# A chunked recurrence in four strands, with its group norm done chunk by chunk

## The chip, the cores and the metric

The kernel runs on one core of a Trainium2 chip. The metric is the device time of one execution in microseconds (us). Of the core's engines, PE (TensorE) multiplies matrices, DVE (VectorE) and ACT (ScalarE) do the elementwise work, POOL (GpSimd) does a few small powers, and SP issues the DMAs. Each engine takes its instructions strictly in the order in which the compiled program lists them for it.

## The reference

A decoder trunk of two layers over 1024 tokens of width 1024, in float32. The first layer mixes time with a linear recurrence (RWKV-7), the second with differential attention; each is followed by a gated feed-forward layer with a short convolution. What the change touches is the recurrence of the first layer and the group norm on its output:

```
def step(state, inp):
    rt, wt, kt, vt, at, bt = inp
    sa = jnp.einsum('bhvk,bhk->bhv', state, at)
    state = state * wt[:, :, None, :] + sa[..., None] * bt[:, :, None, :] + vt[..., None] * kt[:, :, None, :]
    y = jnp.einsum('bhvk,bhk->bhv', state, rt)
    return state, y
...
mean = jnp.mean(o, axis=-1, keepdims=True)
var = jnp.mean(jnp.square(o - mean), axis=-1, keepdims=True)
o = ((o - mean) * lax.rsqrt(var + GN_EPS)).reshape(bsz, s, d) * ln_w + ln_b
bonus = jnp.sum(rh * kh * r_k.astype(jnp.float32), axis=-1, keepdims=True) * vh
o = o + bonus.reshape(bsz, s, d)
return (o * g).astype(h.dtype) @ w_o, v_first
```

There are 16 heads of 64. The state of a head is 64 x 64.

## The kernel before

The 1024 tokens of the recurrence are cut into 8 tiles of 128, and a tile into 4 chunks of 32. Within a chunk the recurrence is solved in matrix form, so only the state goes from chunk to chunk. A tile has six parts, each a generator that yields between its steps:

- `wkv_e` (10 steps): loads, decays, keys. It writes the buffers `AS` (two) and `KB` (one).
- `wkv_a` (7 steps): first four steps, one for each chunk, that form the products `KB` x `AS` on PE (L625) and mask them on DVE (L631, L636); then the inverse of a 32 x 32 triangle for each head and chunk: a run of 28 small DVE instructions (L653, L655), transposes that give `TT` (L662), and two products on PE (L671, L677) with an ACT copy between them. It is called "the solve" here.
- `wkv_x`, "the turn" (4 steps): DVE scales `KD` by the decay (L688), PE multiplies it by `KB` (L696), ACT copies the result into `KD` (one buffer, which the chain reads).
- `wkv_c`, "the chain" (4 chunks x 3 steps): the products with the state, L723, L732, L745 and L753, with an ACT copy behind each. L753 gives the output, which goes to `YT`.
- `wkv_p` (4 steps): group norm of the whole tile (square on ACT L768, sum on DVE L770, power on POOL L307, scaling on DVE L773), transposes on PE (L778), bias and gate (L782 to L793), store.

`wkv` sets their order: `wkv_e` and `wkv_a` of the next tile (front, 17 steps) are woven one step for one with `wkv_c` and `wkv_p` of the present one (back, 16 steps), and when both are done the turn of the next tile follows alone. All products of e, a, x and p go through three PSUM banks (tag `w`), those of the chain through two others.

Beside all this runs a filler, the generator `beside`: the second half of the projections (matmuls `ps<-xh`), then the output projection of finished tiles (`ps<-oh`), then `ffn_pre`, the up-projection of the feed-forward layer for the first half (`u<-h`). The driver in `trunk` gives it 0.4 of a step for each step of the recurrence while the projections last and until tile 4 is done, then 0.75 of a step. What is left is drained after the recurrence, together with the output projection of the second half.

A scheduler then fixes the order on each engine: mostly program order, with instructions of neighbouring steps moved past each other.

Of the kernel before, what the change touches and what calls it, by code (L numbers as in the profile page):

```python
# [9 lines left out]
F32 = mybir.dt.float32  # L10
F32R = mybir.dt.float32r
BF16 = mybir.dt.bfloat16
AF = mybir.ActivationFunctionType
ALU = mybir.AluOpType
AX = mybir.AxisListType
PSUM = bass.MemoryType.PSUM

P = 128
S = 1024
D = 1024  # L20
NK = 8
# [6 lines left out]
GN_EPS = 64e-5  # L28
# [45 lines left out]
def EG(nc, i):  # L74
    return nc.gpsimd if i in EP else nc.vector
# [10 lines left out]
class Trunk:  # L86
# [421 lines left out]
    def wkv_e(self, T):  # L508

        nc = self.nc  # L510
# [4 lines left out]
        wk, we = self.wk, self.we  # L515
        cst = self.wcst
# [7 lines left out]
        bv = T.bv = wk.tile([P, NK, P], F32, tag="bv", name="bv", bufs=2)  # L524
        nc.sync.dma_start(bv, self.rkv_d[2, half, :, :, qs].rearrange("j p t -> p j t"))
        AS = T.AS = wk.tile([P, 2, NK, 4, 64], F32, tag="AS", name="AS", bufs=2)
        KB = T.KB = wk.tile([P, NK, 4, 64], F32, tag="KB", name="KB")
        PC = T.PC = wk.tile([P, 2, NK], F32, tag="PC", name="PC", bufs=2)
        inv = wk.tile([P, 16], F32, tag="inv", name="inv")

# [5 lines left out]
        for jh in range(2):  # L536
# [29 lines left out]
            sq = et("tz")  # L566
# [20 lines left out]
                nc.tensor.matmul(bo[:, jj * P:(jj + 1) * P], self.bork[:, 4 * jh + jj, :], rk[:, jj, :], start=True, stop=True)  # L587
            for b in range(2):
                nc.vector.tensor_copy(PC[:, b, js], E1[:, b::2, 64])
            kbd = KB[:, js, :, :].rearrange("p j c t -> p (j c) t")  # L590
            EG(nc, 2).tensor_tensor(out=kbd[:, :, 0:32], in0=c4(kp), in1=c4(E3), op=ALU.mult)
            for hh in range(2):
# [22 lines left out]
    def wkv_a(self, T):  # L615

        nc, wk, cst = self.nc, self.wk, self.wcst
        AS, KB, NA = T.AS, T.KB, self.NA
        for c in range(4):
            Ap = self.wtile_ps()  # L620
            for j in range(NK):
                for hh in range(2):
                    r = slice(64 * hh, 64 * hh + 64)
                    o = slice(64 - 64 * hh, 128 - 64 * hh)
                    nc.tensor.matmul(Ap[o, j * 64:(j + 1) * 64], KB[r, j, c, :], AS[r, hh, j, c, :], start=True, stop=True)  # L625
            Av = Ap.rearrange("p (j t) -> p j t", j=NK)
            for hh in range(2):
                u0 = 96 - 64 * hh
                for jp in range(2):
                    g = 3 - 2 * hh - jp  # L630
                    nc.vector.tensor_tensor(  # L631
                        out=NA[32 * g:32 * g + 32, 4 * c:4 * c + 4, :], in0=Av[u0:u0 + 32, jp::2, 0:32],
                        in1=cst[u0:u0 + 32, W_NM:W_NM + 32].unsqueeze(1).to_broadcast([32, 4, 32]), op=ALU.mult)
            for hh in range(2):
                o = slice(64 - 64 * hh, 128 - 64 * hh)
                nc.vector.tensor_tensor(out=AS[o, hh, :, c, :], in0=Av[o], in1=cst[o, W_AM:W_AM + 64].unsqueeze(1).to_broadcast([64, NK, 64]), op=ALU.mult)  # L636
            yield

        even, first = cst[:, W_M0:W_M0 + 1], cst[:, W_M0 + 1:W_M0 + 2]
        tr = lambda t: t.rearrange("p s (b t) -> p t (s b)", t=16)  # L640
        n2 = lambda: wk.tile([P, 16, CH], F32, tag="NT", name="NT", bufs=2)
        Nn = wk.tile([P, 16, CH], F32, tag="Nn", name="Nn")
        NT = n2()
        nc.vector.transpose(NT, tr(NA))
        M = wk.tile([P, 16, 16], F32, tag="M", name="M")
        nc.vector.scalar_tensor_tensor(out=M, in0=NT[:, :, 0:16], scalar=even, in1=NT[:, :, 16:32], op0=ALU.mult, op1=ALU.add)
        nc.vector.transpose(Nn, NA)
        tmp = wk.tile([P, 64], F32, tag="tmp", name="tmp")

        for j in range(1, 15):  # L650
            a = 15 - j
            tv = tmp[:, :a * j].rearrange("p (x y) -> p x y", x=a)
            nc.vector.tensor_tensor(out=tv, in0=M[:, j + 1:, j:j + 1].to_broadcast([P, a, j]),  # L653
                                    in1=M[:, j:j + 1, :j].to_broadcast([P, a, j]), op=ALU.mult)
            nc.vector.tensor_tensor(out=M[:, j + 1:, :j], in0=M[:, j + 1:, :j], in1=tv, op=ALU.add)  # L655
        nc.vector.memset(M.rearrange("p a b -> p (a b)")[:, ::17], 1.0)

        DX = n2()
        nc.vector.tensor_scalar(out=DX[:, :, 0:16], in0=M, scalar1=even, scalar2=None, op0=ALU.mult)
        nc.vector.tensor_tensor(out=DX[:, :, 16:32], in0=M, in1=DX[:, :, 0:16], op=ALU.subtract)  # L660
        TT = T.TT = wk.tile([P, 16, CH], F32, tag="TT", name="TT", bufs=2)
        nc.vector.transpose(tr(TT), DX)  # L662
        DN = n2()
        nc.vector.transpose(DN, TT)
        yield
        ps = [self.wtile_ps(), self.wtile_ps()]
        Rs = wk.tile([P, 256], F32, tag="Rs", name="Rs")
        for i in range(16):
            for g in range(4):
                r = slice(32 * g, 32 * g + 32)  # L670
                nc.tensor.matmul(ps[0][r, 16 * i:16 * i + 16], Nn[r, i, :], TT[r, i, 16:32], start=True, stop=True)  # L671
        nc.scalar.copy(Rs, ps[0][:, 0:256])
        yield
        for i in range(16):
            for g in range(4):
                r = slice(32 * g, 32 * g + 32)
                nc.tensor.matmul(ps[1][r, 16 * i:16 * i + 16], DN[r, i, :], Rs[r, 16 * i:16 * i + 16], start=True, stop=True)  # L677
        nc.vector.scalar_tensor_tensor(out=TT[:, :, 16:32], in0=ps[1][:, 0:256].rearrange("p (s t) -> p s t", t=16), scalar=first,
                                       in1=TT[:, :, 16:32], op0=ALU.mult, op1=ALU.add)
        yield  # L680

    def wkv_x(self, T):
# [7 lines left out]
        for c in (0, 2, 1, 3):  # L690
            Kp = self.wtile_ps()
            for j in range(NK):
                for hh in range(2):
                    r = slice(64 * hh, 64 * hh + 64)
                    o = slice(64 - 64 * hh, 128 - 64 * hh)
                    nc.tensor.matmul(Kp[o, j * 64:(j + 1) * 64], T.KB[r, j, c, :], KD[r, hh, c, j, :], start=True, stop=True)  # L696
            for hh in range(2):
# [12 lines left out]
    def wkv_c(self, T):  # L710

        nc, wk = self.nc, self.wk
        AS, TT, KD = T.AS, T.TT, self.KD
        fl = lambda t: t.rearrange("p a b -> p (a b)")
        YT = T.YT = wk.tile([P, 4, 256], F32, tag="YT", name="YT")
        self.wkv_v(T.ti, 0)
        for c in range(4):
            s0, s1 = self.svu[c % 2], self.svu[1 - c % 2]
# [31 lines left out]
            for jj in range(2):  # L750
                for hh in range(2):
                    for j4 in range(4):
                        nc.tensor.matmul(Yp[32 * j4:32 * j4 + 32, (jj * 2 + hh) * 64:(jj * 2 + hh) * 64 + 64],  # L753
                                         AS[:, hh, jj * 4 + j4, c, 32:64], s0[:, hh, jj * 4 + j4, :], start=True, stop=True)
            nc.scalar.copy(YT[:, c, :], Yp[:, 0:256])
            yield

    def wkv_p(self, T):

        nc, wk, we = self.nc, self.wk, self.we  # L760
        YT, bv = T.YT, T.bv
        gl0, gl1 = T.lot[2], T.lot[3]
        ptile = self.wtile_ps
        y3 = YT.rearrange("p c (h v) -> p (c h) v", v=64)
        var = wk.tile([P, 16], F32, tag="st", name="st")
        bcs = lambda a: a.unsqueeze(2).to_broadcast([P, 16, 64])
        sq = we.tile([P, 16, 64], F32, tag="gq", name="gsq")
        nc.scalar.activation(sq, y3, AF.Square)  # L768
        yield
        nc.vector.tensor_reduce(out=var, in_=sq, axis=AX.X, op=ALU.add)  # L770
        self.rstd_cols(var, var, 64, GN_EPS)
        yield
        nc.vector.tensor_tensor(out=y3, in0=y3, in1=bcs(var), op=ALU.mult)  # L773
        on = we.tile([P, NK, P], F32, tag="gq", name="on")
        for jj in range(2):
            tp = ptile()
            for c in range(4):
# [18 lines left out]

    def wkv(self):

        class Tile:
            pass  # L800
        ts = []
        for i in range(8):
            t = Tile()
            t.ti = i
            ts.append(t)
        self.tiles_done = 0

        def front(t):
            yield t.ti // 4 + 1
            for g in (self.wkv_e(t), self.wkv_a(t)):  # L810
                for _ in g:
                    yield 0

        def back(t):
            for g in (self.wkv_c(t), self.wkv_p(t)):
                for _ in g:
                    yield 0
            self.tiles_done += 1

        def turn(t):  # L820
            for _ in self.wkv_x(t):
                yield 0
        yield from front(ts[0])
        yield from turn(ts[0])
        for i, t in enumerate(ts):
            yield from weave(back(t), front(ts[i + 1]) if i < 7 else iter(()), 16, WF)
            if i < 7:
                yield from turn(ts[i + 1])


    def x_open(self, half, right=False):
# [741 lines left out]
END = object()  # L1573
# [7 lines left out]
def weave(a, b, na, nb):  # L1581

    da = db = 0
    la = lb = True
    while la or lb:
        if la and (not lb or da * nb <= db * na):
            v = next(a, END)
            la = v is not END
            da += 1
        else:  # L1590
            v = next(b, END)
            lb = v is not END
            db += 1
        yield 0 if v is END else v
# [79 lines left out]
WF = 17  # L1674
# [186 lines left out]
```

## Time and profile before

| | |
|---|---|
| median of 3 runs | 3306.48 us (3298.51 to 3312.58) |
| the profiled execution | 3304.96 us, its span 3303.2 us |
| the recurrence | from about 320 to 1240 us of the span |
| PE, DVE, ACT busy over the span | 91%, 65%, 37% |
| mean granted clock of PE | 0.943 of 2.4 GHz |

The span is the time from the first instruction to the last. A wait is idle time of an engine, put down to the instruction that ended it. The granted clock has two levels, 1.2 and 2.4 GHz; a mean of 0.89 says that 22% of a stretch ran at the lower one.

### The profile page before, as it was taken

To read this page: it belongs to the slowest core of one execution; us is meant where nothing else is said; L and a number is where in the kernel's file an instruction comes from. 1 tells how busy PE (TensorE), PEld (TensorE's weight loads), DVE (VectorE), ACT (ScalarE), POOL (GpSimd) and SP (SyncE) were. 2 spreads that over 40 slices of the span, in tenths; PEclk is the share of its full clock that TensorE was granted. 3 is DMA by queue.
4 is the path that set the end of the run, shared out by engine and by line. 5 is a ranking of instruction groups with operands and counts; after the bars stand their busy time and mean duration, and the time that the engine had idled before them with its cause. 6 is when DMAs were issued, how large, how long until landed. Compare 5 with 4: busy or idle time off the path is not lost.

```text
span 3303.2 us, 53483 instructions
## 1 busy us (share of the span) xinstructions
PE 3004.2 (91%) x21607; PEld 2419.4 (73%) x21607; DVE 2152.5 (65%) x3752; ACT 1228.2 (37%) x2165; POOL 84.1 (3%) x50
## 2 busy tenths in 40 slices
PE   5988888987899997899999889898889999999997
PEld 2574667776677775788888678787678888888885
DVE  2656778566777855687777676777656655555555
ACT  3634455554454543322223333444333221222123
POOL 0000000000000000000000000000000000000000
PEclk7999899988899998999999899899899999999998
DMA  7363344343433337454443445445552111111111
GB/s 244 113 201 111 98 125 122 115 116 109 117 116 106 100 105 241 153 159 138 141 153 121 149 134 141 136 124 153 151 177 97 52 51 39 58 45 51 39 45 51
DMA packets 441402, 387.85 MB, mean 117 GB/s; under 512 B 42832, under 2 KB 369856, under 8 KB 440130
## 3 DMA queue, kind: packets, MB, share of 16 engines
q1 hardware_dynamic: 438850, 380.23, 38.3%
q8 instruction: 170, 2.79, 0.4%
q10 hardware_dynamic: 2304, 4.20, 0.3%
q14 instruction: 78, 0.64, 0.1%
HBM read 298.74 MB, written 83.49 MB: 116 GB/s over the span
## 4 chain that ended last, share of the span: by engine, by line
PE 68%; DVE 14%; DMA 6%; issue 6%; ACT 4%; POOL 1%; SPq 0%; DVEq 0%; POOLq 0%; ACTq 0%
PE u L109 9%; PE u L110 8%; PE u L111 8%; PE d L109 5%; PE d L111 5%; PE d L110 5%; PE ps L109 5%; PE ps L110 4%; PE ps L111 4%; DMA agw<-in_ada_w_dram 2%; PE wp L696 1%; PE sc L1539 1%; PE cp L745 1%; DVE AS L636 1%; PE tp L1466 1%
## 5 line engine op out<-in xcount | busy, mean ns | idle before, releaser
L109 PE MATMUL u<-h,whl 128*128 128x512 f32 x1408 | 561.8, 399 | 12.7 <-DVE mu L1089 10.0
L110 PE MATMUL u<-h,whl 128*128 128x512 f32 x1408 | 554.3, 394 | 6.2 <-DVE whl L164 6.2
L111 PE MATMUL u<-h,whl 128*128 128x512 f32 x1408 | 552.7, 393 | 0.0
L1134 DVE SCALAR_TENSOR_TENSOR x<-d,mod,x 128x512 f32<-128x512 f32 x352 | 261.8, 749 | 180.7 <-PE d L111 180.6
L109 PEld LDWEIGHTS u<-h,whl 128*128 128x128 f32 x1408 | 265.7, 189 | 73.5 <-ACT h L1090 10.2
L110 PEld LDWEIGHTS u<-h,whl 128*128 128x128 f32 x1408 | 265.8, 189 | 63.3 <-DVE whl L164 8.7
L111 PEld LDWEIGHTS u<-h,whl 128*128 128x128 f32 x1408 | 265.6, 189 | 59.6
L100 ACT CAST whl<-raw 128x1024 fp32r<-128x1024 f32 x140 | 143.9, 1042 | 433.6 <-PE d L111 421.5
L1046 DVE SCALAR_TENSOR_TENSOR a<-u,cwc,a 128x511 f32<-128x511 f32 (+1 forms) x132 | 122.0, 924 | 258.7 <-ACT a L1045 258.6
L109 PE MATMUL d<-hid,whl 128*128 128x512 f32 x704 | 280.1, 398 | 8.3 <-ACT hid L100 6.0
L110 PE MATMUL d<-hid,whl 128*128 128x512 f32 x704 | 277.3, 394 | 0.0
L111 PE MATMUL d<-hid,whl 128*128 128x512 f32 x704 | 275.4, 394 | 0.0
L1045 ACT ACTIVATE a<-u,cwc 128x512 f32<-128x512 f32 (+1 forms) x132 | 121.5, 921 | 390.9 <-PE u L111 390.5
L164 DVE TENSOR_TENSOR whl<-wraw,whl 128x512 fp32r<-128x512 f32 x232 | 158.0, 685 | 123.5 <-ACT whl L163 121.1
L163 ACT CAST whl<-wraw 128x512 fp32r<-128x512 f32 x232 | 142.7, 618 | 248.5 <-PE ps L111 102.9
L109 PE MATMUL ps<-xh,whl 128*128 128x512 f32 x384 | 162.7, 424 | 9.8 <-ACT xh L100 8.2
L101 DVE TENSOR_TENSOR whl<-raw,whl 128x1024 fp32r<-128x1024 f32 x140 | 168.9, 1217 | 4.0 <-ACT whl L100 3.8
L109 PEld LDWEIGHTS d<-hid,whl 128*128 128x128 f32 x704 | 133.2, 189 | 44.4 <-ACT hid L100 9.3
L111 PE MATMUL ps<-xl,whl 128*128 128x512 f32 x384 | 156.7, 409 | 4.6 <-DVE xl L101 4.3
L110 PE MATMUL ps<-xh,whl 128*128 128x512 f32 x384 | 156.4, 408 | 4.4 <-DVE whl L164 4.4
L111 PEld LDWEIGHTS d<-hid,whl 128*128 128x128 f32 x704 | 133.2, 189 | 30.3 <-DVE hid L101 1.6
L110 PEld LDWEIGHTS d<-hid,whl 128*128 128x128 f32 x704 | 133.3, 189 | 26.8
(279 smaller groups left out, 5863.9 us busy)
## 6 DMA issues: line engine op xcount, KB each, us to landing
raw<-in_ffn_w_up_dram SPq DMA_DIRECT2D x88, 512.0 KB
wraw<-in_a_w_rkv_dram SPq DMA_DIRECT2D x96, 256.0 KB
agw<-in_ada_w_dram SPq DMA_DIRECT2D x96, 256.0 KB
wraw<-in_ffn_w_up_dram SPq DMA_DIRECT2D x88, 256.0 KB
raw<-in_ffn_w_down_dram SPq DMA_DIRECT2D x44, 512.0 KB
agw<-in_ada_w_dram SPq DMA_DIRECT2D x128, 128.0 KB
rkv_d<-st SPq DMA_DIRECT2D x48, 256.0 KB
wraw<-in_a_w_o_dram SPq DMA_DIRECT2D x48, 256.0 KB
```

The costliest lines, as they stand in the source:

```text
L100: nc.scalar.copy(h, src)
L101: nc.vector.tensor_tensor(out=l, in0=src, in1=h.bitcast(F32), op=ALU.subtract)
L109: nc.tensor.matmul(ps, wh, xh, start=first, stop=False)
L110: nc.tensor.matmul(ps, wl, xh, start=False, stop=False)
L111: nc.tensor.matmul(ps, wh, xl, start=False, stop=last)
L163: nc.scalar.copy(wt[:, 0], raw)
L164: self.low().tensor_tensor(out=wt[:, 1], in0=raw, in1=wt[:, 0].bitcast(F32), op=ALU.subtract)
L636: nc.vector.tensor_tensor(out=AS[o, hh, :, c, :], in0=Av[o], in1=cst[o, W_AM:W_AM + 64].unsqueeze(1).to_broadcast([64, NK, 64]), op=ALU.mult)
L696: nc.tensor.matmul(Kp[o, j * 64:(j + 1) * 64], T.KB[r, j, c, :], KD[r, hh, c, j, :], start=True, stop=True)
L1045: nc.scalar.activation(a, u, AF.Identity, bias=c[3], scale=c[2])
L1046: nc.vector.scalar_tensor_tensor(out=a[:, 1:], in0=u[:, :n - 1], scalar=c[1], in1=a[:, 1:], op0=ALU.mult, op1=ALU.add)
L1134: nc.vector.scalar_tensor_tensor(out=xs, in0=ps, scalar=gate[:, j:j + 1], in1=xs, op0=ALU.mult, op1=ALU.add)
```

## The change

The inverse becomes a generator of its own, `wkv_s` (3 steps), and `wkv` runs four strands in turn, a step of each that can go: back (chain, then `wkv_p`), solve, turn and front (`wkv_e`, then the four steps of `wkv_a`). A strand goes on as soon as what it needs is done or its buffer is free; the front of a tile may start two steps before the turn of the tile ahead of it has released `KB`. The norm moves into the chain: after each chunk its 128 x 256 outputs are squared, summed, raised to -1/2 and scaled. The steps of a tile fall from 38 to 35, and with them the filler's share.

```diff
@@ wkv_e
-        KB = T.KB = wk.tile([P, NK, 4, 64], F32, tag="KB", name="KB")
...
+            if jh == 0:
+                KB = T.KB = wk.tile([P, NK, 4, 64], F32, tag="KB", name="KB")
@@ wkv_a
             yield
+
+    def wkv_s(self, T):
+
+        nc, wk, cst, NA = self.nc, self.wk, self.wcst, self.NA
@@ wkv_c
+        var = wk.tile([P, 4, 4], F32, tag="st", name="st")
+        on = T.on = self.we.tile([P, NK, P], F32, tag="gq", name="on")
+        bv4 = lambda t: t.rearrange("p (h v) -> p h v", v=64)
...
             nc.scalar.copy(YT[:, c, :], Yp[:, 0:256])
+
+            sq = bv4(on[:, 2 * c:2 * c + 2, :].rearrange("p a b -> p (a b)"))
+            nc.scalar.activation(sq, bv4(YT[:, c, :]), AF.Square)
+            nc.vector.tensor_reduce(out=var[:, c], in_=sq, axis=AX.X, op=ALU.add)
+            self.rstd_cols(var[:, c], var[:, c], 64, GN_EPS)
+            nc.vector.tensor_tensor(out=bv4(YT[:, c, :]), in0=bv4(YT[:, c, :]), in1=var[:, c].unsqueeze(2).to_broadcast([P, 4, 64]),
+                                    op=ALU.mult)
             yield
@@ wkv_p
-        sq = we.tile([P, 16, 64], F32, tag="gq", name="gsq")
-        nc.scalar.activation(sq, y3, AF.Square)
-        yield
-        nc.vector.tensor_reduce(out=var, in_=sq, axis=AX.X, op=ALU.add)
-        self.rstd_cols(var, var, 64, GN_EPS)
-        yield
-        nc.vector.tensor_tensor(out=y3, in0=y3, in1=bcs(var), op=ALU.mult)
@@ wkv
-        yield from front(ts[0])
-        yield from turn(ts[0])
-        for i, t in enumerate(ts):
-            yield from weave(back(t), front(ts[i + 1]) if i < 7 else iter(()), 16, WF)
-            if i < 7:
-                yield from turn(ts[i + 1])
+        def front():
+            for i, t in enumerate(ts):
+                while done["p"] < i - 1 or self.halves < i // 4 + 1:
+                    yield False
+                for n, _ in enumerate(self.wkv_e(t)):
+                    yield True
+
+                    while n == 1 and done["x"] < i:
+                        yield False
+                done["e"] += 1
...
+        def turn():
+            for i, t in enumerate(ts):
+                while done["e"] <= i or done["c"] < i:
+                    yield False
+                for _ in self.wkv_x(t):
+                    yield True
+                done["x"] += 1
+
+        def solve():
+            for i, t in enumerate(ts):
+                while done["a"] <= i:
+                    yield False
...
+        def back():
+            for i, t in enumerate(ts):
+                while done["s"] <= i or done["x"] <= i:
+                    yield False
...
+        live = [back(), solve(), turn(), front()]
```

The first place at which the orders are compared is PE's queue at the end of tile 3 (`AS,KB` are the products of `wkv_a` for tile 4, `YT` the transposes of `wkv_p`, `TT,Nn` and `Rs,NT` the solve, `KD,KB` the turn, `lot` with `w2x` or `a2a` the first products of the next front, `ps<-oh` the filler). Before:

```order
L625 MATMUL wp<-AS,KB 64x64 x32
L723 MATMUL cp<-svu_1980,AS 32x64 x16
L778 MATMUL wp<-cst,YT 128x128 x8
...
L671 MATMUL wp<-TT,Nn 32x16 x64
...
L677 MATMUL wp<-Rs,NT 32x16 x64
...
L696 MATMUL wp<-KD,KB 64x64 x6
...
L696 MATMUL wp<-KD,KB 64x64 x16
...
L544 MATMUL wp<-lot_2000,w2x 128x128 x4
```

With the change, at the same place:

```order
L761 MATMUL cp<-svu_1981,AS 32x64 x16
...
L626 MATMUL wp<-AS,KB 64x64 x16
L782 MATMUL wp<-cst,YT 128x128 x8
...
L701 MATMUL wp<-KD,KB 64x64 x16
L626 MATMUL wp<-AS,KB 64x64 x16
...
L701 MATMUL wp<-KD,KB 64x64 x16
...
L543 MATMUL wp<-lot_2000,w2x 128x128 x4
L546 MATMUL wp<-lot_2001,a2a 128x128 x4
...
L701 MATMUL wp<-KD,KB 64x64 x16
L731 MATMUL cp<-svu_1980,AS 32x64 x16
...
L676 MATMUL wp<-TT,Nn 32x16 x13
```

The turn's 64 products and the first products of the next front stood behind both products of the solve; they stand ahead of them now, with 11 to 25 filler matmuls between them. At the ends of the other tiles one to three of the four groups of the turn are ahead of the solve's second product, and the next front follows the third group or the last.

The second place is DVE's queue at the same tile end (`st` and `YT` are the norm, `NA` and `AS` the masking of `wkv_a`, `KD` the turn, L644 the start of the solve). Before:

```order
L770 TENSOR_REDUCE st<-gsq 128x16
L631 TENSOR_TENSOR NA<-wp,wcst 32x128
L306 TENSOR_SCALAR st<-st 128x16
L631 TENSOR_TENSOR NA<-wp,wcst 32x128 x3
L636 TENSOR_TENSOR AS<-wp,wcst 64x8x64 x2
L773 TENSOR_TENSOR YT<-YT,st 128x1024
L644 STREAM_TRANSPOSE NT<-NA 128x512
```

With the change:

```order
L637 TENSOR_TENSOR AS<-wp,wcst 64x8x64 x2
L767 TENSOR_REDUCE st<-on 128x4
L693 TENSOR_TENSOR KD<-wcst,PC 64x512
L306 TENSOR_SCALAR st<-st 128x4
L693 TENSOR_TENSOR KD<-wcst,PC 64x512
L769 TENSOR_TENSOR YT<-YT,st 128x256
L632 TENSOR_TENSOR NA<-wp,wcst 32x128 x4
```

The last chunk's norm now stands after the masking of the first of four chunks instead of the last. Between the sum and the scaling of a chunk, over all 32 of them, the order has none to three rows of other DVE work besides L306, and once eight.

## Rows read from the trace of the kernel before

**Rows 1.** The page: PE's busy share; the clock granted in 40 slices.

```profile
PE 3004.2 (91%) x21607; PEld 2419.4 (73%) x21607; DVE 2152.5 (65%) x3752; ACT 1228.2 (37%) x2165; POOL 84.1 (3%) x50
...
PEclk7999899988899998999999899899899999999998
```

**Rows 2.** Busy time by stretch: start:end, length, PE, PEld, DVE, ACT, POOL, clock, DMA.

```profile
320.00:860.00 540.00, 457.61 (x6999) 378.12 (x6998) 377.50 (x810) 280.09 (x581) 35.59 (x16) 0.89 0.39 113
860.00:1240.00 380.00, 357.70 (x4337) 287.76 (x4336) 274.88 (x587) 193.94 (x374) 20.55 (x8) 0.97 0.36 108
1240.00:1340.00 100.00, 72.54 (x288) 56.02 (x287) 54.50 (x82) 34.09 (x55) 1.01 (x1) 0.82 0.73 231
```

**Rows 3.** The same by 20 us, around two tile ends.

```profile
540.00:560.00 20.00, 15.85 (x226) 11.13 (x224) 18.68 (x38) 11.46 (x19) 3.28 (x1) 0.88 0.23 68
...
580.00:600.00 20.00, 18.26 (x442) 16.29 (x443) 3.73 (x8) 9.50 (x17) 0.00 (x0) 0.91 0.31 94
...
740.00:760.00 20.00, 11.32 (x183) 10.73 (x180) 18.69 (x43) 6.91 (x16) 2.89 (x1) 0.83 0.22 62
760.00:780.00 20.00, 12.20 (x335) 10.96 (x336) 10.47 (x33) 4.31 (x10) 0.00 (x0) 0.66 0.39 113
```

**Rows 4.** PE's waits from 320 to 1250 us: total, times, longest.

```profile
PE wp L778 <- DVE YT L773: 23.8, 5, 8.3
PE wp L671 <- DVE TT L662: 11.0, 7, 7.4
PE wp L677 <- issue: 10.1, 8, 1.6
```

**Rows 5.** Groups by form: the tile's norm, and the nearest smaller shapes.

```profile
L768 ACT ACTIVATE gsq<-YT 128x1024 f32<-128x1024 f32 x8 | 8.5, 1061 | 0.2
L849 ACT ACTIVATE sq<-xs 128x256 f32<-128x256 f32 x14 | 5.8, 416 | 6.6 <-DVE xs L896 6.4
...
L770 DVE TENSOR_REDUCE st<-gsq 128x16 f32<-128x1024 f32 x8 | 9.7, 1207 | 4.8 <-ACT gsq L768 4.8
L773 DVE TENSOR_TENSOR YT<-YT,st 128x1024 f32<-128x1024 f32 x8 | 9.8, 1219 | 12.4 <-POOL st L307 12.4
L850 DVE TENSOR_TENSOR acc<-acc,sq 128x256 f32<-128x256 f32 x14 | 5.9, 421 | 1.7 <-ACT sq L849 1.6
L306 DVE TENSOR_SCALAR st<-st 128x16 f32<-128x16 f32 x8 | 1.3, 168 | 0.1
...
L307 POOL TENSOR_TENSOR st<-st,mh 128x16 f32<-128x16 f32 x8 | 24.7, 3088 | 265.9 <-DVE st L306 265.9
L307 POOL TENSOR_TENSOR rs<-rs,mh 128x4 f32<-128x4 f32 x10 | 10.1, 1011 | 952.4 <-DVE rs L306 915.4 <-DVE mod L271 37.0
```

**Rows 6.** The turn: its groups on PE and ACT, and tile 0's on PE's timeline.

```profile
L696 PE MATMUL wp<-KD,KB 64*64 64x64 f32 x1024 | 45.0, 260 | 0.8 <-issue 0.7
...
L699 ACT COPY KD<-wp 64x512 f32<-64x512 f32 x64 | 37.1, 580 | 31.6 <-PE wp L696 30.8
...
385.33 6.20 PE L696 MATMUL wp<-KD,KB 64*64 64x64 f32 x113 [0.69 <-issue]
```

**Rows 7.** DVE's waits from 340 to 860 us: for a front's first result.

```profile
DVE tz L563 <- ACT tz L550: 19.1, 5, 9.2
```

**Rows 8.** PE's timeline: a filler matmul at either clock.

```profile
556.78 0.63 PE L110 MATMUL ps<-xh,whl 128*128 128x512 f32 x1
...
569.04 0.39 PE L110 MATMUL ps<-xh,whl 128*128 128x512 f32 x1
```

**Rows 9.** PE's timeline behind the recurrence: the first matmul of the output projection.

```profile
1256.09 0.79 PE L109 MATMUL ps<-oh,whl 128*128 128x512 f32 x1 [9.52 <-ACT oh L100]
```

**Rows 10.** The chain of waits: the store of the last tile.

```profile
1247.37 4.24 DMA o_d<-on
```

**Rows 11.** A power on POOL, and a DVE instruction that starts while it runs.

```profile
609.97 1.95 POOL L581 TENSOR_TENSOR inv<-inv,mh 128x8 f32<-128x8 f32 x1 [53.90 <-DVE inv L580]
...
610.34 0.69 DVE L164 TENSOR_TENSOR whl<-wraw,whl 128x512 fp32r<-128x512 f32 x1
```

More of the change, by code (lines that the diff above doesn't have):

```diff
@@ L760, in wkv_p @@
         nc, wk, we = self.nc, self.wk, self.we
-        YT, bv = T.YT, T.bv
+        YT, bv, on = T.YT, T.bv, T.on
         gl0, gl1 = T.lot[2], T.lot[3]
         ptile = self.wtile_ps
-        y3 = YT.rearrange("p c (h v) -> p (c h) v", v=64)
-        var = wk.tile([P, 16], F32, tag="st", name="st")
-        bcs = lambda a: a.unsqueeze(2).to_broadcast([P, 16, 64])
-        sq = we.tile([P, 16, 64], F32, tag="gq", name="gsq")
-        nc.scalar.activation(sq, y3, AF.Square)
-        yield
-        nc.vector.tensor_reduce(out=var, in_=sq, axis=AX.X, op=ALU.add)
-        self.rstd_cols(var, var, 64, GN_EPS)
-        yield
-        nc.vector.tensor_tensor(out=y3, in0=y3, in1=bcs(var), op=ALU.mult)
-        on = we.tile([P, NK, P], F32, tag="gq", name="on")
         for jj in range(2):
@@ L806, in wkv @@
         self.tiles_done = 0
[L808 to L811, printed above, removed]
-                    yield 0
[L814 to L822, printed above, removed]
-        yield from front(ts[0])
-        yield from turn(ts[0])
@@ L825, in wkv @@
-        for i, t in enumerate(ts):
-            yield from weave(back(t), front(ts[i + 1]) if i < 7 else iter(()), 16, WF)
-            if i < 7:
-                yield from turn(ts[i + 1])
+        done = {n: 0 for n in "eaxscp"}
+        def front():
[7 more added lines that the diff above has]
+                done["e"] += 1
+                for _ in self.wkv_a(t):
+                    yield True
+                done["a"] += 1
@@ new lines, in turn @@
+        def turn():
[3 more added lines that the diff above has]
+                for _ in self.wkv_x(t):
+                    yield True
+                done["x"] += 1
[3 more added lines that the diff above has]
+                    yield False
+                for _ in self.wkv_s(t):
+                    yield True
+                done["s"] += 1
+        def back():
+            for i, t in enumerate(ts):
+                while done["s"] <= i or done["x"] <= i:
+                    yield False
+                for _ in self.wkv_c(t):
+                    yield True
+                done["c"] += 1
+                for _ in self.wkv_p(t):
+                    yield True
+                done["p"] += 1
+                self.tiles_done += 1
@@ L831, in x_open @@
+        live = [back(), solve(), turn(), front()]
+        while live:
+            went = False
+            for g in list(live):
+                v = next(g, END)
+                if v is END:
+                    live.remove(g)
+                elif v:
+                    went = True
+                    yield 0
+            if not went and live:
+                yield 2
     def x_open(self, half, right=False):
```

## The prediction

> **What bounds the kernel now.** I began with the page: PE is busy for 91% of the span, no other engine for more than 65%, and the granted clock is below full in most slices of the first half [rows 1]. So PE's idle time and its slow stretches are all there is to win. The table by stretch shows where they lie. From 320 to 860 us PE is busy for 457.6 of 540, which leaves 82 us idle at a mean clock of 0.89; from 860 to 1240 it idles 22 of 380 at 0.97; in the 100 us behind the recurrence it idles 27 at 0.82 [rows 2]. The first of these stretches has the projections and the output projection as filler, the second `ffn_pre`.
>
> Cut into 20 us, the first stretch shows a pattern that comes back at each tile end. DVE is full (18.7 of 20) while PE idles for 4 to 9 us and the clock falls; then, in the turn, PE works and DVE has almost nothing to do (3.7 of 20) [rows 3]. In the list of PE's waits the end of a tile shows by name: 23.8 us in five waits for the normed tile, 11.0 us for `TT`, 10.1 us for the copy between the two products of the solve, which the trace lists as "issue" [rows 4]. The rest of the idle time is many short waits for operands of the filler. The reader is to see that two engines take turns at the tile end: DVE's queue holds masking, norm and solve in one piece, and the work that PE could do meanwhile, the turn and the next front, stands behind the solve in PE's queue.
>
> **The change, part by part.** The sum is made against the profiled execution, 3304.96 us; it stands 1.5 us below the median of the runs, which is nothing here.
>
> *Norm by chunks, gain.* Behind the last output, the norm took 1.06 (square) + 1.21 (sum) + 0.17 + 3.09 (power) + 1.22 (scaling) = 6.75 us. For a quarter of the columns the nearest rows are 0.42 for the square, 0.42 for an elementwise 128 x 256 on DVE, which I take for both the sum and the scaling, and 1.01 for a power of 128 x 4: 0.42 + 0.42 + 0.17 + 1.01 + 0.42 = 2.44 [rows 5]. That is 4.3 us less between the last output and the transposes. Five waits less 4.3 each is 21.5, but they are uneven and some are shorter than that; I take 18 of the 23.8. Bounds: 9, if the queue ahead of the last scaling on DVE is what is late, and 23.8.
>
> *Norm by chunks, cost.* DVE's own work on it goes from 2.6 us a tile to 4 x (0.42 + 0.17 + 0.42) = 4.0, so 11 us over 8 tiles. ACT's goes from 1.06 to 1.66 us a tile, 5 us in all, hidden, since ACT is at half load in both stretches [rows 2]. POOL's goes from 24.7 to 32 x 1.01 = 32.3 us [rows 5]. It is idle otherwise, but DVE waits for it: 12.4 of the 24.7 us were waited for before [rows 5]; at the same half it is 16, so 4 more. The 15 us on DVE lie on the path where DVE is full, about half of the time: 8 us. Bounds 0 and 20. A tile's first square also waits now for the store of the tile before, 4.2 us [rows 10], since it writes into the stored buffer; the turn and two steps of the chain lie between, so 0, and up to 4 us of ACT's queue a tile without them. SP has the same DMAs as before, the next front's loads a little earlier. If the cover on DVE is gone, what stands behind the scaling in DVE's queue is late: the masking for the solve and the low halves of the filler's weights, for which PE waits.
>
> The Trainium skill has a rule against this part ("SBUF — State Buffer", section "Who interferes with whom"): a DVE instruction with two SBUF inputs and a GpSimd instruction that reads SBUF exclude each other for a whole instruction. By it, all of POOL's 32.3 us could stop DVE, 7.6 more than before, and the sum would be at most 8 us higher. The trace speaks against it: a subtraction of two SBUF operands began 0.37 us into a power of 1.95 us and took its usual 0.69 [rows 11]. I go by the row.
>
> *The solve's waits.* The transposes, or a group of the turn, now stand at and between the two products. A group of the turn costs PE 45.0/32 = 1.4 us [rows 6], as long as the mean "issue" wait (10.1/8 = 1.3) [rows 4], so I take 8 of the 10.1. Of the 11.0 for `TT`, 7.4 are one wait, at the end of tile 3, where the compared orders put the whole turn, the next front's first products and dozens of filler matmuls ahead of the solve: 7 of 11. Together 15; bounds 6 and 21.
>
> *The turn beside the solve.* The turn is 5.6 us of PE a tile [rows 6], and for that time the next front was held, with DVE starved: five waits for a front's first result make 19.1 us, one of 9.2 [rows 7]. Now one to four of its four groups run under the solve. In the first stretch, where DVE's full slices set the pace, I count half of it, 2.8 us, for four tile ends: 11. In the second stretch PE is 94% busy and the filler hides it: 0. Tile 0's turn, 6.2 us with nothing beside it [rows 6], now runs among the products of `wkv_a`: 6. Bounds for both: 0 and 28 (5.6 for each of four, and 6).
>
> *Clock.* From 320 to 860 us a mean of 0.89 means 22% at 1.2 GHz, 119 us. A filler matmul takes 0.63 us there against 0.39 [rows 8]. Nearly all of the 82 us of idle time lies in or at those stretches, so some 60 us of them are work that would take 30 to 37. The terms above remove about half of the idle time they name in this stretch, and I let a third to a half of the slow stretches go with it: 10. Bounds 0 and 25.
>
> *Behind the recurrence.* A tile now has 35 steps for 38, so some of `ffn_pre` is left over: the new order puts 12 of its matmuls around the last products of `wkv_p` and 175 beside the output projection. The first of that projection waited 9.5 us for its operands [rows 9]; 12 matmuls of 0.39 cover 4.7. I take 5, bounds 0 and 12. Leftover work is only moved.
>
> Sum: -18 - 15 - 11 - 6 - 10 - 5 + 8 = -57, so 3305 - 57 = **3248 us**. All low ends give -15 + 20, 3310; all high ends -110, 3195.
>
> **The rivals.**
>
> *The troughs close.* If the strands keep both engines fed, the first stretch idles like the second: 22/380 of 540 is 32 us, so 50 saved. With a clock of 0.97, most of the 22 to 30 us of the clock term comes too, 25, and some 20 from the later stretches: 95, so 3210 us. For it: DVE has 30% to spare in every stretch [rows 2]. Against it: DVE is already full where PE idles, the solve still stands there, and the bursts of operand splitting for the projections fall on the same place.
>
> *The banks take it back.* Transposes, front, turn and masking share three PSUM banks, and the solve holds two of them across its copy. A group of the turn then waits for the group before it to be copied out, 2 x 0.58 us [rows 6]: 8 tiles x 3 x 1.16 = 28, so 3276 us. For it: four groups had three banks before and ran back to back. Against: filler matmuls use other banks and stand between the groups.
>
> *No change.* The solve on DVE sets a tile's length whatever stands on PE meanwhile; PE's wait for the norm only moves to `TT`. Then what is left is tile 0 and the tail, 11 us, less the 8: 3302 us. For it: DVE's full slices. Against: DVE's empty slices follow directly, and the order does move the next front up.
>
> *Slower.* DVE goes through its queue in order, and 32 times it now meets a sum that waits for a chunk's product, copy and square, then a scaling that waits for POOL. Where the real times differ from those that set the order, DVE stands still, with the filler's weights behind it. At 3 us a chunk this is 96 us, of which 8 are counted: 3305 - 57 + 88 = 3336 us. It decides from (57 + 8 + 16)/32 = 2.5 us a chunk. For it: two of the eight sums of before waited 4.8 us in all for the square [rows 5]. Against: the order has other DVE work between most pairs.
>
> **How the numbers follow.** I give my forecast 0.48, the closed troughs 0.15, the banks 0.15, no change 0.13 and slower 0.09. A change of 0.5% (16.5 us) is about what a measurement of this kernel can tell from none. The first three are faster by more: 0.78; within: 0.13; slower: 0.09. The range goes from the high ends, 3195, to 3308, which takes in the banks and most of no change and leaves out the slower case and some of both edges. The forecast's own range is 3225 to 3270.
>
> **What would show it.** In the profile of the change: the wait of the transposes for `YT` down from 23.8 to about 6 us, that of the solve's products from 21 to about 6; the turn's groups under DVE's solve instead of behind it; the mean clock of the first stretch at 0.92 or more; 32 powers of about 1.0 us. The prediction is wrong if DVE's waits for POOL and for the square come to more than about 40 us, if new waits of L701 or L782 for a bank appear, or if the filler's waits for its operands grow by as much as the named ones shrink.

## The result, and the profile after

The change takes 3255.89 us (median of four runs, 3251.47 to 3261.03), the kernel before 3307.45 in the same comparison: a ratio of 0.9844, with a 95% interval of 0.9823 to 0.9864. That is 51.6 us less, inside the range and 8 us above the forecast. The profiled execution has a span of 3251.2 us and a mean clock of 0.952.

The cleanest comparison is the stretch from 320 us to the first down-projection of the feed-forward layer (`d<-hid`), since both kernels do the same matmuls in it. First the kernel before, by stretch (columns as in [rows 2]): it and the two slices around tile 0's turn.

```profile
320.00:1316.00 996.00, 873.90 (x11573) 710.98 (x11571) 693.70 (x1456) 500.73 (x1000) 56.14 (x24) 0.92 0.41 121
340.00:360.00 20.00, 12.24 (x91) 7.08 (x91) 18.56 (x38) 11.07 (x18) 0.00 (x0) 0.76 0.13 42
380.00:400.00 20.00, 17.62 (x388) 15.75 (x387) 4.59 (x10) 11.46 (x25) 0.00 (x0) 0.74 0.07 20
```

The same view of the changed kernel, with the two stretches of [rows 2] and two slices that are still troughs.

```profile
320.00:1273.10 953.10, 855.61 (x11565) 695.97 (x11563) 692.99 (x1524) 502.92 (x1023) 67.13 (x48) 0.94 0.42 127
320.00:860.00 540.00, 469.07 (x7381) 385.55 (x7379) 401.10 (x921) 291.73 (x617) 44.64 (x32) 0.92 0.40 117
860.00:1240.00 380.00, 357.19 (x4065) 287.64 (x4062) 272.47 (x576) 198.08 (x388) 22.49 (x16) 0.98 0.43 130
340.00:360.00 20.00, 18.69 (x221) 13.23 (x221) 18.82 (x39) 14.29 (x24) 0.00 (x0) 1.00 0.17 54
380.00:400.00 20.00, 18.83 (x439) 15.22 (x437) 15.27 (x32) 8.61 (x21) 2.01 (x1) 1.00 0.43 126
740.00:760.00 20.00, 12.83 (x247) 11.09 (x245) 18.36 (x57) 11.80 (x27) 0.00 (x0) 0.74 0.40 120
820.00:840.00 20.00, 9.01 (x139) 6.88 (x140) 18.27 (x38) 10.19 (x19) 1.38 (x1) 0.61 0.44 130
```

The phase is 996.0 - 953.1 = 42.9 us shorter. PE's idle time (length less busy) falls from 122.1 to 97.5, by 24.6; its busy time for the same 11,570 matmuls falls from 873.9 to 855.6, by 18.3. So in these two profiles two fifths of the phase's gain are not waits but the same matmuls at a higher clock (0.94 for 0.92). The troughs, with the low clock in and behind them [rows 3], are fewer: 6 slices of 20 us with more than 4 us of idle time on PE, for 11 before. The mean clock of whole executions, known for every run, says the same: 0.952 to 0.954 in the four runs of the change, 0.942 to 0.948 in 37 runs of the kernel before. The other 9 us lie between the first down-projection and the second layer's output projection, where nothing was changed: 1196.7 before, 1187.7 after. In the fourteen profiles of this study that stretch takes between 1187.7 and 1200.5 us, in no order that follows the kernels' times, so I count those 9 as scatter of a profile. The change's is the shortest of them all, and one profile of each kernel cannot say whether the 51.6 us of the medians lie in the phase alone.

PE's waits from 320 to 1250 us, in the change:

```profile
PE ps L109 <- ACT oh L100: 17.5, 4, 8.6
PE wp L782 <- DVE YT L769: 7.7, 4, 3.2
PE wp L676 <- DVE TT L667: 6.4, 5, 1.9
...
PE wp L701 <- issue: 6.0, 4, 2.2
PE cp L753 <- ACT svu L745: 6.0, 3, 3.3
PE wp L682 <- issue: 5.8, 5, 1.8
...
PE wp L782 <- DVE M L661: 3.0, 2, 1.6
```

Against [rows 4], the transposes' wait for the normed tile goes from 23.8 to 7.7 us and the solve's two waits from 21.1 to 12.2. What is new is 6.0 us ahead of the turn's groups (L701; 0.7 before), for which the profile names no releaser, and 3.0 ahead of the transposes while DVE is in the solve. The transposes do not read `M`, and in both of these rows the scaling of `YT` had ended 0.15 us before, just as in the four that bear its name; so they are the same wait, 10.7 us in all. The first row is the output projection waiting for its operand. Of its 17.5 us, 8.6 lie behind the recurrence (shown below), at a place that falls outside this window in the kernel before; over the whole phase it is 17.5 for 12.2.

DVE's waits in the same stretch:

```profile
DVE whl L164 <- ACT whl L163: 30.2, 37, 1.9
DVE YT L769 <- POOL st L307: 27.4, 31, 2.0
...
DVE st L767 <- ACT on L766: 12.1, 11, 4.2
...
DVE tz L562 <- ACT tz L549: 7.8, 4, 3.3
```

In the kernel before, the first and the last of these were:

```profile
DVE whl L164 <- ACT whl L163: 82.7, 47, 7.5
DVE tz L563 <- ACT tz L550: 21.0, 8, 9.2
```

DVE waits 52.5 us less for ACT's half of the filler's weights; what that is worth on PE no run separates. The scaling waits 27.4 us for POOL where it waited 12.4, and the sum 12.1 for the square where it waited 4.8 [rows 5]: 39.5 for 17.2. DVE's order fits this: 0 to 2 of its instructions stand between L306 and the scaling in all 32 chunks, where it was 18 to 24 in three of the eight tiles before and 5 or fewer in the others. The chunk norm itself costs what was estimated; by form:

```profile
L766 ACT ACTIVATE on<-YT 128x256 f32<-128x256 f32 x32 | 13.4, 419 | 0.8
L767 DVE TENSOR_REDUCE st<-on 128x4 f32<-128x256 f32 x32 | 13.2, 414 | 12.5 <-ACT on L766 12.1
L769 DVE TENSOR_TENSOR YT<-YT,st 128x256 f32<-128x256 f32 x32 | 13.6, 425 | 27.4 <-POOL st L307 27.4
L307 POOL TENSOR_TENSOR st<-st,mh 128x4 f32<-128x4 f32 x32 | 36.1, 1130 | 359.7 <-DVE st L306 349.2 <-DVE mod L291 10.6
```

How the turn now stands under the solve is seen on PE's timeline at the end of tile 2 (start, duration; L676 and L682 are the solve, L701 the turn, whose first group runs while DVE is in the 28 small instructions):

```profile
637.95 1.15 PE L701 MATMUL wp<-KD,KB 64*64 64x64 f32 x32
...
649.96 1.25 PE L676 MATMUL wp<-TT,Nn 32*32 32x16 f32 x128 [0.64 <-DVE TT L667]
651.13 1.15 PE L701 MATMUL wp<-KD,KB 64*64 64x64 f32 x32
...
653.96 0.99 PE L682 MATMUL wp<-Rs,NT 32*32 32x16 f32 x97 [0.88 <-issue]
654.89 1.14 PE L701 MATMUL wp<-KD,KB 64*64 64x64 f32 x31
```

Behind the recurrence, the first matmul of the output projection still waits nearly as long as in [rows 9]:

```profile
1179.18 0.80 PE L109 MATMUL ps<-oh,whl 128*128 128x512 f32 x1 [8.55 <-ACT oh L100]
```

### The profile page after: what moved, and what is told of

It is laid out like the page before. It is cut to its first block, busy times and chain, and to the rows that moved or that the text cites. A ratio compares the mean times of both kernels' runs of the same rounds, so it can differ in the third digit from the quotient of the medians.

```text
span 3251.2 us, 53634 instructions
## 1 busy us (share of the span) xinstructions
PE 2984.1 (92%) x21607; PEld 2400.7 (74%) x21607; DVE 2154.7 (66%) x3824; ACT 1231.3 (38%) x2189; POOL 95.1 (3%) x74
## 4 chain that ended last, share of the span: by engine, by line
PE 57%; DVE 9%; issue 5%; DMA 2%; ACT 2%; POOL 0%; SPq 0%; DVEq 0%; POOLq 0%; ACTq 0%
PE u L109 9%; PE u L111 9%; PE u L110 9%; PE d L109 5%; PE d L111 5%; PE d L110 5%; PE ps L109 3%; PE ps L110 3%; PE ps L111 3%; PE sc L1577 1%; PE tp L1504 1%; PE sc L1578 1%; DVE mx L1582 1%; DVE pd L1596 1%; DMA wraw<-in_ffn_w_up_dram 1%
## 5 line engine op out<-in xcount | busy, mean ns | idle before, releaser
L110 PEld LDWEIGHTS d<-hid,whl 128*128 128x128 f32 x704 | 133.4, 189 | 27.1
```

What stands on the lines that cost most here:

```text
L110: nc.tensor.matmul(ps, wl, xh, start=False, stop=False)
```

## The experiments

Twelve kernels were run in three lots, each lot beside the kernel before on its chip. "Phase" is the stretch from 320 us to the first down-projection in the profiled execution, with PE's busy and idle time in it; "POOL" is DVE's wait in it for the power ahead of the norm's scaling. The kernel before took 3308.55, 3312.10 and 3311.30 us in the three lots, so kernels of different lots are compared by their ratios; a difference of 0.001 is 3.3 us. A profile is one execution, and some lie off their kernel's median: 5 us below it with the turn behind the solve, 7 above for the strands with the norm once a tile and for "both of these", 11 above for "the same, norm once a tile" and 14 in the last row. So a few microseconds of busy or idle time between two rows of the table mean nothing by themselves.

| kernel | median us | ratio to before, interval | phase | busy | idle | POOL |
|---|---|---|---|---|---|---|
| before | 3307.45 | 1 | 996.0 | 873.9 | 122.1 | 12.4 |
| the change | 3255.89 | 0.9844 (0.9823 to 0.9864) | 953.1 | 855.6 | 97.5 | 27.4 |
| strands, norm once a tile | 3255.99 | 0.9837 (0.9816 to 0.9859) | 961.4 | 866.9 | 94.5 | 14.1 |
| weave, norm by chunks | 3287.03 | 0.9932 (0.9917 to 0.9947) | 979.1 | 867.8 | 111.3 | 30.6 |
| turn behind the solve | 3283.68 | 0.9923 (0.9907 to 0.9939) | 973.1 | 873.9 | 99.2 | 26.8 |
| solve at the front's end | 3278.99 | 0.9903 (0.9885 to 0.9921) | 969.7 | 876.4 | 93.3 | 29.6 |
| both of these | 3276.62 | 0.9909 (0.9892 to 0.9925) | 971.7 | 864.7 | 107.0 | 24.7 |
| more filler a step | 3262.69 | 0.9853 (0.9838 to 0.9868) | 954.6 | 864.4 | 90.2 | 26.4 |
| solve in one bank | 3264.46 | 0.9859 (0.9844 to 0.9874) | 967.3 | 870.8 | 96.5 | 27.5 |
| the same, norm once a tile | 3260.16 | 0.9850 (0.9830 to 0.9870) | 965.9 | 870.4 | 95.5 | 14.2 |
| norm a chunk late | 3264.27 | 0.9859 (0.9845 to 0.9872) | 957.3 | 865.5 | 91.8 | 23.1 |
| change, two powers | 3298.28 | 0.9965 (0.9952 to 0.9978) | 993.6 | 873.5 | 120.1 | 59.6 |
| before, two powers | 3328.66 | 1.0061 (1.0046 to 1.0075) | 1015.4 | 875.6 | 139.8 | 27.1 |
| strands, tile norm, two powers | 3283.22 | 0.9924 (0.9903 to 0.9945) | 987.5 | 871.7 | 115.8 | 35.6 |

### The two halves of the change, each alone

**Strands with the norm once a tile.** The chunk norm is taken out of `wkv_c`, and `wkv_p` is that of before:

```diff
@@ wkv_c
-            nc.scalar.activation(sq, bv4(YT[:, c, :]), AF.Square)
-            nc.vector.tensor_reduce(out=var[:, c], in_=sq, axis=AX.X, op=ALU.add)
...
@@ wkv_p
+        nc.scalar.activation(sq, y3, AF.Square)
+        yield
+        nc.vector.tensor_reduce(out=var, in_=sq, axis=AX.X, op=ALU.add)
...
```

> The four strands as in the change, but the group norm once a tile in wkv_p, as before. My theory (the terms of the prediction, each on its own): the norm's 18 us come back less the 8 us that its chunks cost, so about 10 us slower than the change: 3262 to 3270. Rival A, the gain is the shorter norm chain and the strands only move work: 3290 or more. Rival B, the chunked norm costs DVE what it saves PE: 3250 to 3258, no different from the change.

**The weave with the norm by chunks.** The same lines the other way round, in the kernel before.

> The weave and the separate turn as before, but the group norm by chunks (14 steps of the back against 17 of the front). My theory: only the norm's term, 18 less 8, and a little of the shorter step count: 3290 to 3298. Rival A (the norm is what pays): 3265 or less. Rival B (the chunks cost what they save): 3303 to 3320.

The strands alone give all of it, 0.9837 against 0.9844; the chunk norm alone gives 0.68%, 22 us. So the two do not add: given the strands, the chunk norm is worth nothing that can be measured. My expectation for the first was wrong, and its rival B came true; the second came out 3 us better than my range. The reason by name is in PE's waits. With the strands and the tile norm the transposes wait only

```profile
PE wp L783 <- DVE YT L778: 6.5, 3, 2.7
```

and in the weave with the chunk norm

```profile
PE wp L777 <- DVE YT L764: 7.1, 5, 2.3
```

where they waited 23.8 us before: either half removes most of the same wait.

### What in the strands does it

**The turn only behind the solve**, with strands and chunk norm left as they are:

```diff
-                while done["e"] <= i or done["c"] < i:
+                while done["s"] <= i or done["c"] < i:
```

> The change, but the turn of a tile may begin only when the solve of that tile is done, as it was before; the solve keeps its own strand. My theory: the turn's 17 us and a part of the solve's waits (5 or more, since nothing stands between its two products) come back: 3274 to 3284. Rival (the turn's place is worth nothing, the solve on DVE sets a tile's length): 3250 to 3262.

**The solve at the end of the front strand**, with no strand of its own:

```diff
                 done["a"] += 1
+                for _ in self.wkv_s(t):
+                    yield True
+                done["s"] += 1
...
-        live = [back(), solve(), turn(), front()]
+        live = [back(), turn(), front()]
```

> The change, but the solve is the end of the front strand again, so the next front cannot start until the solve is done; the turn still runs beside it. My theory: the turn beside the solve is what counts, the early front only a few us: 3256 to 3266. Rival (the strands pay because the next front starts early): 3275 or more.

**Both edits together:**

> The change with the solve as the end of the front strand and the turn only behind the solve, so that only a strand that holds front and solve, one for the turn and one for the chain are left. Theory (the two edits save the same thing: PE's and DVE's other work beside the tile end, so either one undone already loses most of it): ratio 0.990 to 0.994, the weave with the norm by chunks, where each alone has 0.990 and 0.992. Rival (the two add up, 28 and 23 us): 0.9844 + 51/3308 = 1.000, so 0.997 to 1.002.

Each edit costs most of what the strands add to the chunk norm: 0.79% and 0.59%, 26 and 20 us, and both together 0.65%, 21 us, where the whole way from the change back to the weave with the chunk norm is 0.88%, 29 us. So this is one gain with two conditions, as expected of the third run. The conditions are in the code: the next front runs beside the solve only if the turn has gone early (it frees `KB`, without which the front stops behind its second step) and the solve does not stand in the front's strand. The traces agree: with the solve at the front's end the first tile's turn still ran from 333 to 357 us, ahead of its solve at 381, and yet the time is that of both edits. So the early turn by itself is worth nothing that these runs can tell. No run had the front early and the turn late, which would take a second `KB`; to that extent the reading of the two conditions is argued. I underrated the second; "early front" had been a side effect to me.

How it is lost was not expected either. The phase of the two single edits, first the turn's, then the solve's:

```profile
320.00:1293.10 973.10, 873.88 (x11565) 713.53 (x11565) 693.18 (x1524) 504.16 (x1023) 68.08 (x48) 0.92 0.42 124
```

```profile
320.00:1289.70 969.70, 876.44 (x11567) 712.43 (x11567) 697.82 (x1526) 503.17 (x1023) 72.15 (x48) 0.92 0.42 125
```

PE idles 99.2 and 93.3 us, no more than the change's 97.5. It is busy 18.3 and 20.8 us longer with the same matmuls: the mean clock is 0.92 instead of 0.94. In these two profiles the loss is slow matmuls, not a longer idle time, and the clock of all runs agrees: 0.943 to 0.950 and 0.945 to 0.949 over whole executions, for 0.952 to 0.954 in the change. With both edits the one profile has it half and half (9.5 idle, 9.1 busy). Why the clock is lower in the two is open: they have no more idle time in total, and no more slices of 20 us with over 4 us of it (6 each).

### Filler and banks

**More filler a step**, 38/35 of what the change takes, so that a tile takes as much as before:

```diff
-NS0 = 0.4
-NSM = 0.4
+NS0 = 0.434
+NSM = 0.434
...
-NS1 = 0.75
+NS1 = 0.814
```

> The change with each step of a tile taking 38/35 of the filler it takes now (0.434 for 0.4, 0.814 for 0.75), so that 35 steps take as much as 38 did. Theory (the gain is the order of the strands; how much filler stands beside a tile matters little, leftover work is only moved): within 8 us of the change's 3256. Rival (the smaller share left the tiles with too little filler and the tail with more): 3235 to 3246, PE's busy time from 320 to 1340 us at 930 or more. Other rival (the smaller share is itself part of the gain, since less filler stands ahead of the solve in the queues): 3266 or more.

It is 0.9853 and makes no difference. The last solve comes later, at 1135.4 us for 1110.6 (the start of its last DVE instruction, as in what follows), and the first down-projection at 1274.6 instead of 1273.1: leftover filler is only moved, as the prediction had it. This also explains a trap. The recurrence, from the first solve to the eighth, takes 722.8 us in the change and 743.2 in the strands with the tile norm, which looks like a gain of 20 us for the chunk norm. But the latter has 37 steps a tile for 35, and with the filler evened out the change takes 1135.4 - 393.8 = 741.6.

**The solve's two products in one bank**, once in the change and once in the strands with the tile norm:

```diff
-        ps = [self.wtile_ps(), self.wtile_ps()]
+        pb = self.wtile_ps()
+        ps = [pb[:, 0:256], pb[:, 256:512]]
```

> The change with the two products of the solve in the two halves of one PSUM bank in place of two banks. Theory (the new waits of the turn and of the transposes, 6.0 us at L701 and 3.0 at L782, are hardly the banks): within 6 us of the change's 3256. Rival (the banks hold the turn back): the waits of the turn's products and of the second product of the solve go from 12 us to under 5, and the time to 3240 to 3249. Slower, 3262 or more, if the second product, which now shares a bank with one that is being copied out, has to wait for that copy longer than it did.

> The strands with the norm once a tile as before, and the solve's two products in one bank. By the theory (banks of no account) it comes out with the strands under the tile norm, 3256, within 6 us. By the rival (banks hold the strands back) 3240 to 3249, like the same edit under the chunk norm.

0.9859 and 0.9850: no gain from a bank set free, and 0.13 to 0.15% more than without the edit, within the intervals. In microseconds the first, 3264, lies in the range that I gave for slower, but its condition is not met: the second product's wait is 5.2 us for 5.8. The turn's wait stays at 6.2 us for 6.0. So those new waits are not the solve's hold on two of the three banks.

### What the wait for POOL costs

**The norm one chunk late** for chunks 0 to 2, to take DVE's 39.5 us of waits out of its way:

```diff
             nc.scalar.copy(Ws, Wp[:, 0:256])
+            if c:
+                norm(c - 1)
             yield
...
                 self.wkv_v(T.ti, c + 1)
+            if c:
+                scale(c - 1)
             yield
```

> The change with the norm of chunks 0 to 2 issued one chunk later: square, sum and power at the first step of the next chunk, the scaling at its second; chunk 3 as in the change. Theory (DVE's 39.5 us of waits for POOL and for the square take back what the chunk norm gives): these waits fall to under 20 us, and the time to 3238 to 3248. Rival (those waits lie where PE has other work, and the norm's place adds nothing once the strands are there): within 6 us of 3256, though the waits fall.

DVE's waits hardly fell:

```profile
DVE YT L776 <- POOL st L307: 23.1, 29, 1.2
...
DVE st L772 <- ACT on L771: 11.9, 10, 4.2
```

35.0 for 39.5 us, since the scheduler still puts the scaling close behind the power: none to three DVE instructions stand between L306 and it in 31 of the 32 chunks. The time, 0.9859, says nothing about the cost then, for my theory or its rival, and the next three runs lengthen the wait instead.

**Two powers for each one**, the first into a tile that nothing reads, in the change, in the kernel before and in the strands with the tile norm. The scheduler knows of the second power and shifts some rows, so the order differs a little too.

```diff
+        if junk is not None:
+            nc.gpsimd.tensor_tensor(out=junk, in0=out, in1=self.mh.to_broadcast(list(out.shape)), op=ALU.pow)
         nc.gpsimd.tensor_tensor(out=out, in0=out, in1=self.mh.to_broadcast(list(out.shape)), op=ALU.pow)
```

> The change with a second power of 128x4 on POOL ahead of each of the 32 (into a tile that nothing reads), so that each chunk's scaling is released some 1.0 us later. Theory (DVE's waits for POOL, 27.4 us in the change, lie where PE has other work in its queue): DVE's wait grows to 50 us or more, and the time stays within 8 us of the change, ratio to before 0.982 to 0.987. Rival (DVE's queue is on the path and the chunk norm holds it back): 32 times 1.0 us, a half to all of it, so 16 to 32 us more, ratio 0.989 to 0.994.

> The kernel before with a second power of 128x16 on POOL, 3.09 us, ahead of each of its eight. Theory (in the weave the norm's chain ends the wait at five tile ends): PE's wait for YT grows from 23.8 to some 35 us or more, and the time by 10 to 25 us, ratio 1.003 to 1.0075. Rival (the waits for the norm were not on the path either, and the chunk norm gained in the weave by something else): within 4 us, 0.999 to 1.001.

> The strands with the norm once a tile, with the same second power of 128x16. Theory (the strands put the turn and the next front's products under the norm, so its length does not matter): within 6 us of the same kernel without it, ratio 0.982 to 0.9855. Rival (the norm's chain still sets five or more tile ends): 10 to 25 us more than without it, ratio 0.987 to 0.991.

My theory fell in the first and the third, and the cost in both lies beyond even the rival's range. In the second the time came out as expected. The second power costs the change 1.21%, 40 us, for 32.2 us more of DVE's wait for POOL; the strands with the tile norm 0.87%, 29 us, for 21.5; the kernel before 0.61%, 20 us, for 14.7. By the intervals these costs are known to within 5 to 10 us. DVE's wait in the change with two powers, then the phase:

```profile
DVE YT L772 <- POOL st L309: 59.6, 32, 2.5
```

```profile
320.00:1313.60 993.60, 873.48 (x11564) 710.84 (x11563) 693.18 (x1524) 502.42 (x1023) 100.57 (x80) 0.92 0.40 122
```

The 40 us show in the phase as 22.6 more idle and 17.9 more busy. So a longer wait of DVE for POOL is not covered in any of the three: each microsecond of it costs 1.2 to 1.4, the shifted rows included. That is the price of lengthening it. What the 27.4 us cost that are there in the change no run shows, since the norm a chunk late did not remove them. One reason for the price may be that the filler is given out by steps, not by time, so a longer tile brings no more of it; no run tests this.

PE's list of waits shows only a part of the cost. The transposes wait, over the phase, in the change, in the kernel before and in the strands with the tile norm, each with two powers:

```profile
PE wp L785 <- DVE YT L772: 13.8, 4, 4.8
PE wp L785 <- DVE M L663: 5.8, 2, 3.3
...
PE wp L781 <- DVE YT L776: 31.7, 6, 11.2
...
PE wp L786 <- DVE YT L781: 15.4, 3, 5.6
```

That is 19.6 us for 10.7, 31.7 for 23.8 and 15.4 for 6.5: 8 to 9 us more each time, of 40, 20 and 29; in the second I had expected 35 or more. The rest came out under other names and as slower matmuls; the filler's operands behind the scaling in DVE's queue are where I would look.

The traces with two powers also bear on the rule on POOL and DVE. The sums over the phase say little: DVE's 1524 instructions take 693.18 us with 100.57 us of POOL beside them, and 692.99 us with 67.13, but in most of the 33.4 us more DVE was only waiting. The subtractions of [rows 11] say more. In the change with two powers 12 of the 232 lay for more than half of their time under a power on POOL, and took 0.689 us on the mean; the other 220 took 0.685. The Trainium skill ("SBUF — State Buffer", section "Who interferes with whom") has the two engines exclude each other when DVE reads two operands from SBUF and GpSimd reads there too; these durations show nothing of it. What the traces show of POOL's cost is the wait for its result.

## Why the prediction was right, point by point

**The sum** was right, 3248 for 3256, but partly by luck, since its parts are off on both sides. The terms on waits came to 47 us, their cost taken off, and the clock to 10; the phase shows 24.6 of idle time and 18.3 of clock. The waits gave about half of what I allowed and the clock nearly twice, though the mean clock of the first stretch came out as foretold (0.92). What brings the profile's 52 us near my 57 is the 9 us outside the phase, which no term names.

**The norm, -18 and +8.** The transposes' wait fell by 16.1 us by its name (13.1 with the rows named after `M`), for the 18 foretold, and the instructions cost what was estimated (0.42 us each, powers of 1.13 for 1.01). In the weave the term is worth 22 us, with the shorter step count in it, more than the 10 that I gave. In the change it is worth nothing that can be measured, and the strands remove most of the same wait by themselves. Adding it to the strands' terms was the step that failed. The cost was too small: I took half of POOL's time as waited for, 4 us more than before; DVE waits for it 15 us more, and 7 us more for the square, and the runs with two powers show that more of such waiting costs at least its length. A gain from the shorter chain that this cost takes back would fit what was measured, but no run separates the two.

**The solve's waits, -15, and the turn, -17.** For the strands behind the chunk norm this makes 32; the weave with the chunk norm to the change measures 29, in which a share of the clock is contained. The named waits fell by only 8.9 us, not 15, and the turn's waits took 5.3 back (6.0 for 0.7). Tile 0 is the clear part: its turn now runs among the products of `wkv_a`, and from 340 to 360 us PE is busy 18.7 us instead of 12.2, and full clock instead of 0.76; with the slice from 380 on that is 7.7 us of idle time, for the 6 foretold. The DVE wait for a front's first result went from 21.0 to 7.8 us from 320 to 1250, but it is 7.3 to 9.3 us also in the three kernels that lose most of the strands' gain again, so it is no measure of that gain. What I had not seen is that turn and solve must both move for either to pay.

**Behind the recurrence, -5.** This did not come: 9.5 us of wait became 8.6.

**The rivals.** The troughs did not close: 820 to 840 us has PE at 9.0 of 20, at a clock of 0.61, with DVE full. The banks needed 28 us of waits at the turn's groups, which wait 6.8 us in all, and a bank set free by the solve changed nothing. No change is out by 51.6 us. The slower case has its mechanism in the runs with two powers: DVE held longer at each chunk costs time, 1.2 us for each in the change. Only its size is below the point that decides: 39.5/32 = 1.2 us a chunk for 2.5. Two of my signs of being wrong came close: those 39.5 us, for a bound of about 40, and the new waits at L701 and L782, which the runs in one bank do not trace to the solve's banks.

## What to carry to other kernels

Edits that attack one wait do not add: try each alone before summing their gains, and undo each in turn after. Where the clock moves with the order of the work, compare the busy time of the same matmuls as well as the waits; here it held two fifths of the phase's gain, and nearly all of the loss in the two profiles in which half of the reordering was undone. And the cost of a wait is not what the row that bears its name on the bounding engine grows by, here 8 to 9 us of 20 to 40: lengthen it on purpose and see what the end does. Look at such a row over the whole phase: in the kernel before with two powers it is 31.7 us, but 23.8 in a window that ends at 1250 us, ahead of the last tile's norm, which would have looked like no difference at all.

## What the runs showed of the hardware

A power on POOL took 1.13 us for 128x4 on the mean and 2.00 for 128x8 here, so four of a quarter (4.5) took more than one of 128x16 (3.09 in the kernel before). A subtraction of two 128x512 operands took hardly longer under such a power (0.689 us for 0.685). PE's granted clock fell to 0.61 in a slice in which PE was busy 9.0 of 20 us, and stood at 1.00 in one in which it was busy 18.7. The same 11,570 matmuls took between 855.6 and 876.4 us in the fourteen profiles, by the order of the work and by scatter between executions, of which one profile of each kernel does not give the shares.
